# A transformer block in split float32: the activations tile H moves behind the small constants

## The chip, the cores and the metric

The kernel runs on one core of one Trainium2 chip. The metric is the device time of one execution in microseconds (us). A matmul here is one TensorE (PE) instruction: its stationary operand (up to 128 columns) is loaded by a weight load (PEld), and then its moving operand (up to 512 columns) is streamed through.

## The reference

One block of a transformer on x[512, 2048], in float32:

```
h    = rms_norm(x, pre_mix_norm)
proj = h @ w_in                          # queries, keys, values, gates
mix  = [diff_attention(8 heads), nsa_attention(8 heads, 2 groups)]
x    = x + rms_norm(mix @ w_out, post_mix_norm)
h    = rms_norm(x, pre_ffn_norm)
u    = causal_dwconv(h @ w_up)           # 2 x 5632 columns, width 3
gate, up = split(u)
y    = (gelu(gate) * up) @ w_down        # 5632 -> 2048
x    = x + rms_norm(y, post_ffn_norm)
```

## The kernel before

Every large product is made of three matmuls on operands split into a high part and a low part (type float32r): high by high, high by low, low by high. ScalarE (ACT) makes the high part with a copy (line 132), VectorE (DVE) the low part with a subtraction (line 133); all matmuls of this kind are issued by the helper mm (line 73).

The tile H holds the activations of a stage, transposed and split: 128 partitions by [2, 16, 512] float32, so 64 KB in each partition. H[:, 0, c] and H[:, 1, c] are the high and the low part of the 128 rows c of the contraction, 2048 bytes per partition each. It is filled four times: with the normed x (lines 202 and 203), with the attention's output (mix_ahead, lines 132 and 133), with the second norm's output (lines 763 and 764), and at the very end with weights of the last part of the down projection (hold_split, lines 132 and 133).

The other operands lie in two pools. "weights" has raw (3 buffers), hi and lo (2 each) of 4096 bytes per partition: raw receives 512 KB of weights by a DMA of SP's queue, hi and lo are its split. "slots" has 37 slots s of 2048 bytes (queries, keys, values, gated activations and much else) and 4 buffers pt of 6656 bytes (13 times 512).

The stages, and which operand H is in each (in `mm(out, stationary, moving)`):

- moving() with the weights wdv, wvs and wvg: H is stationary, the weight tile moves.
- stationary() with wst (queries and keys) and wu (the up projection): the weight tile is stationary, H moves. Between the wst matmuls a queue of small items (scores, transposes, products with values) is worked off; tick() starts one after every few matmuls, so that runs of wst matmuls are broken up. The items of the up projection use no TensorE.
- out_pass() with wo, two token halves: H is stationary, the weight tile moves.
- first_pairs(): the first 4 of the 88 column tiles of the up projection, in pieces of 256 columns.
- down() with wd: the stationary operand is a slot (gated activations), the moving one a weight tile. H takes no part. There are 10 such stages of 192 matmuls, each after a stretch of the up projection.
- The last group of the down projection runs the same down_mms, but its weights lie in H: a slot is stationary, H moves.

The inner loops, all through mm (line 73):

```python
# stationary(): 48 matmuls into one bank
h = hi[:, c * 128:(c + 1) * 128]
mm(b, h, H[:, 0, cc], cc == 0, False)
mm(b, h, H[:, 1, cc], False, False)
mm(b, lo[:, c * 128:(c + 1) * 128], H[:, 0, cc], False, cc == KC - 1)
...
# down_mms(): the slot moves on by token tile, the weights by 2048 bytes
mm(b, gh[:, ts], hi[:, w], first and c == 0, False)
mm(b, gh[:, ts], lo[:, w], False, False)
mm(b, gl[:, ts], hi[:, w], False, last and c == 1)
...
# last_mms(): the same call, hi and lo are now parts of H
hi = H[:, 0, m:m + 2].rearrange("p a b -> p (a b)")
```

Within a pool tiles are laid out in the order in which they are first asked for, each rounded up to 32 bytes. "consts" comes first, and H is its first tile; 15 small constants follow, and gcol is asked for last. The start addresses in a partition (bytes), as the built program has them:

```
tile                          address    mod 2048
H                               16512         128
ident ... vcl, gcol    82048 to 94496     various
raw, hi, lo           94560 to 119136         352
s (37 slots)         123232 to 196960         352
pt (4)               199008 to 218976         352, 864, 1376, 1888
```

Column slices of 128 float32 move a start by 512 bytes, so operands cut from hi, lo, s and pt start at 352 modulo 512 (except some slices of queries of the compressed branch), those cut from H at 128 modulo 512.

Of the kernel before, what the change touches and what calls it, by code (L numbers as in the profile page):

```python
# [13 lines left out]
F = mybir.dt.float32  # L14
R = mybir.dt.float32r
# [6 lines left out]
KC = D // 128  # L22
# [28 lines left out]
def body(ctx, tc, xT, x, gpre, vecs, lam4, tab, onehot, cmpm, wst, wdv, wvs, wvg, w1, w2, wo, wu, wd,  # L51
         gpost, gffn, gpff, out):
    nc = tc.nc
    cp = ctx.enter_context(tc.tile_pool(name="consts", bufs=1))
# [17 lines left out]
    def mm(o, a, b, start, stop):  # L72
        T.matmul(o, a, b, start=start, stop=stop, skip_group_check=True)  # L73

    H = cp.tile([128, 2, KC, 512], R, name="H")
    ident = cp.tile([128, 128], F, name="ident")
    vec = cp.tile([128, V_N], F, name="vec")
    half = cp.tile([128, 4], F, name="half")
# [9 lines left out]
    kcl = cp.tile([128, NKV, 32], R, name="kcl")  # L88
    vch = cp.tile([32, NKV, 128], R, name="vch")
    vcl = cp.tile([32, NKV, 128], R, name="vcl")  # L90
    rv = dp.tile([16, RW], F, name="rv")
    rows_b = dp.tile([16, 128, RW], F, name="rows_b")
    park = dp.tile([PARK, 128, 512], F, name="park")
# [4 lines left out]
    pace = {"rate": 2.0, "credit": 0.0, "now": 0, "ticks": 0, "hold": 0}  # L98

    def step():  # L100
        """one half step: even ones start an item and run second stages, odd ones run the later stages"""
        now = pace["now"] = pace["now"] + 1
        if now % 2:
            run = [f for f in flying if f[1] >= 2 and now - f[2] >= (LAG if f[1] == 2 else 1)]
        else:
            run = [f for f in flying if f[1] == 1]
            if pending and pace["ticks"] >= pace["hold"]:
                run.insert(0, [pending.popleft(), 0, now])
                flying.append(run[0])
        for f in run:  # L110
            f[0][f[1]]()
            f[1] += 1
            f[2] = now
        flying[:] = [f for f in flying if f[1] < len(f[0])]
# [73 lines left out]
                 start=start if k == 0 else None, after=(lambda: evac(box["b"])) if last else None)  # L188
            c0 += n

    # ---- norm of x, transposed and split
    xraw = {}

    def load_x(c0, n):
# [31 lines left out]
            T.transpose(b[:, t * 128:(t + 1) * 128], rstd[:, t:t + 1].to_broadcast([128, 128]), ident)  # L226
        A.activation(rstd_b, b, AF.Copy)

    # ---- tables
    def tables():  # L230
        tb = st.tile([33, 16], F, name="tb")
        oh = sp.tile([33, RW], F, name="oh", tag="pt", bufs=4)
# [32 lines left out]
            V.tensor_copy(kcl[:, :, 31], z)  # L265
        return [bias, lam]

    # ---- evacuations
    def evac_dmajor(scale, hi, lo):
        def f(b):  # L270
            t = slot()
# [4 lines left out]
    LO, UP = slice(0, 64), slice(64, 128)  # L276

    def evac_twins(h, b):
        """keys of the two maps, each twice on the partitions, and their low parts"""
        t = slot()  # L280
        V.tensor_tensor(t, b, rstd_b, OP.mult)
        k0, k1, kl = hold["k", h] = [slot(R) for _ in range(3)]
        A.activation(k0, t, AF.Copy)
        A.activation(k1[UP], t[UP], AF.Copy)
        V.tensor_tensor(kl, t, k0.bitcast(F), OP.subtract)
        nc.gpsimd.dma_start(k0[UP], k0[LO])
        nc.gpsimd.dma_start(k1[LO], k1[UP])

    def evac_stack(h, b):
        """queries of the two maps, high and low parts stacked on the partitions"""  # L290
        t = slot()
        V.scalar_tensor_tensor(t, b, 0.125, rstd_b, op0=OP.mult, op1=OP.mult)
        q0, q1 = hold["q", h] = [slot(R) for _ in range(2)]
        A.activation(q0[LO], t[LO], AF.Copy)
        A.activation(q1[UP], t[UP], AF.Copy)
        V.tensor_tensor(q0[UP], t[LO], q0[LO].bitcast(F), OP.subtract)
        V.tensor_tensor(q1[LO], t[UP], q1[UP].bitcast(F), OP.subtract)
# [7 lines left out]
                V.scalar_tensor_tensor(lo, banks[t][:, :n], r, hi.bitcast(F), op0=OP.mult, op1=OP.subtract)  # L305
        return f

    # ---- attention
    OFF = [0, 384, 768, 1152]
    bias_tiles = {}  # L310

# [4 lines left out]
        bias_tiles[h] = bt  # L316

    def softmax_items(maps, bt, combine, pts):
        """one softmax over the four query tiles; each map is a list of products of queries and keys"""
        zs, nm, sm = {}, {}, {}  # L320

        def scores(i):
            n = 128 * (i + 1)
            qs = slice(i * 128, (i + 1) * 128)
            zs[i] = []
            m = stat(2)
            s = sm[i] = stat(2)
            bs = [bank() for _ in maps]
            for p in range(len(maps[0])):
                for b, ops in zip(bs, maps):  # L330
                    mm(b[:, :n], ops[p][0][:, qs], ops[p][1][:, :n], p == 0, p == len(ops) - 1)
            for j, b in enumerate(bs):
                z = slot()
                zs[i].append(z)
                V.tensor_tensor_reduce(out=z[:, :n], in0=b[:, :n], in1=bt[:, 384 - 128 * i:384 - 128 * i + n],  # L335
                                       scale=-1.0, scalar=3e38, op0=OP.add, op1=OP.min, accum_out=m[:, j:j + 1])
                A.activation(z[:, :n], z[:, :n], AF.Exp, bias=m[:, j:j + 1], scale=-1.0, accum_out=s[:, j:j + 1])  # L337

        def norm(i):
            n = 128 * (i + 1)  # L340
            s = sm[i][:, :len(maps)]
            V.tensor_scalar(s, s, TINY, None, op0=OP.max)
            V.reciprocal(s, s)
            combine(i, n, zs[i], s)

        def turn(i):
            n = 128 * (i + 1)
            o = slice(OFF[i], OFF[i] + n)
            for z, pt in zip(zs.pop(i), pts):
                b = bank()  # L350
                for j in range(i + 1):
                    T.transpose(b[:, j * 128:(j + 1) * 128], z[:, j * 128:(j + 1) * 128], ident)  # L352
                split(pt[0][:, o], pt[1][:, o], b[:, :n])

        return [[lambda i=i: scores(i), lambda i=i: norm(i), lambda i=i: turn(i)] for i in (3, 2, 1, 0)]
# [2 lines left out]
        return [sp.tile([128, 1664], R, name="pt", tag="pt", bufs=4) for _ in range(2)]  # L358

    def weighted(b, vh, vl, pt, first, last):  # L360
        """b[e, q] += v^T p^T over the key tiles"""
        for j in range(NT):
            o = b[:, j * 128:]
            def view(t):
                return t[:, :1664].rearrange("p (a b) -> p a b", b=128)[:, 4 * j:4 * j + 3 * (NT - 1 - j) + 1:3]
            f = first and j == 0
            mm(o, vh(j), view(pt[0]), f, False)
            mm(o, vh(j), view(pt[1]), False, False)
            mm(o, vl(j), view(pt[0]), False, last and j == NT - 1)
# [118 lines left out]
        cl[-1] += [lambda: av(0), lambda: (av(1), done())]  # L488
        return cl

    # ---- phase 1: projections and attention
    make_identity(nc, ident)
    V.memset(half, -0.5)
    A.activation(stat(1), half[:, :1], AF.Exp)
# [2 lines left out]
    wb = bank()  # L497
    for _ in range(3):
        T.matmul(wb, ident, warm, start=True, stop=True)
    gcol = cp.tile([128, KC], F, name="gcol")  # L500
    nc.sync.dma_start(gcol, gpre)
    nc.gpsimd.dma_start(vec, vecs)
    bgl = tables()
# [184 lines left out]
    units[-1]["start"] = lambda: start_out()  # L688
    units[-1]["each"] = lambda n: mix_ahead(n - 1) if n else None

    # ---- phase 2: output projection in two token halves, residual, second norm
    msum = st.tile([128, NT, 4], F, name="msum")
    x2sum = st.tile([128, NT, 4], F, name="x2sum")
    mg = {}
# [115 lines left out]
        if n % 3 != 1:  # L810
            u["start"] = lambda n=n: (early_split if n % 3 else early_fetch)(n // 3)

    # ---- phase 3: gated feed-forward
    conv = {}
    gact = {}
    y = {}
# [91 lines left out]
        early[HELD[e]] = hs, ls  # L908

    def first_pairs():  # L910
        """the first two pairs, on the tokens that are ready first and then on the rest"""
        banks = {}

        def part(key, cols):
            j, which, k = key
            hs, ls = early[key]
            if (j, which) not in banks:
                banks[j, which] = bank()
            b = banks[j, which][:, cols]
            for c in range(8):  # L920
                cc = k * 8 + c
                o = slice(c % 4 * 128, c % 4 * 128 + 128)
                mm(b, hs[c // 4][:, o], H[:, 0, cc, cols], cc == 0, False)
                mm(b, hs[c // 4][:, o], H[:, 1, cc, cols], False, False)
                mm(b, ls[c // 4][:, o], H[:, 0, cc, cols], False, cc == KC - 1)
                if c % 2:
                    yield

        for e in (6, 7):
            def mms(hi, lo, e=e):  # L930
                early[HELD[e]] = [[v[:, o:o + 512] for o in (0, 512)] for v in (hi, lo)]
                for key in HELD[:6] if e == 6 else []:
                    yield from part(key, slice(0, 256))
                yield from part(HELD[e], slice(0, 256))

            def start():
                pace["rate"] = 1.0

            def after():
                flush()  # L940
                for key in HELD:
                    for _ in part(key, slice(256, 512)):
                        pass
                early.clear()
                pace["rate"] = 2.0
                for j in range(2):
                    for which in range(2):
                        up_evac(j, which)(banks.pop((j, which)))
                rows.clear()
            j, which, k = HELD[e]  # L950
            unit(wu[(j * 2 + which) * 2 + k], 1024, mms, start=start if e == 6 else None, after=after if e == 7 else None)
            units[-1]["late"] = e == 7
# [8 lines left out]
            if G and j == G * GROUP:  # L961
                down(G - 1)

    # ---- the weight stream
    raws, his = {}, {}

    def fetch(i):
# [83 lines left out]
    while deferred:  # L1051
        deferred.pop(0)()

    # ---- last group of the down projection, token tiles outermost; its weights take the place of the activations
    gp = row(gpff)
    hold_fetch(2)
    for m in range(4):
# [76 lines left out]


def _halves(w, k=8):
    """[2048, n * 128] to [n * 2, 128, 8 * 128]: column tiles with the rows of a half on the partitions"""
    n = w.shape[1] // 128
    return w.reshape(2, 8, 128, n, 128).transpose(3, 0, 2, 1, 4).reshape(n * 2, 128, 1024)

# [45 lines left out]
```

## Time and profile before

| what | value |
|---|---|
| time, median of 2 runs | 2373.7 us (2372.87 to 2374.53) |
| profiled execution, first to last instruction | 2371.7 us |
| matmuls | 10956, PE busy 2346.8 us (99%) |
| weight loads | PEld busy 1914.7 us (81%) |
| VectorE, ScalarE, GpSimd busy | 54%, 38%, 4% |
| mean granted TensorE clock | 0.998 of full speed |

The profiled span stands beside the median with 2.0 us between them, which lie outside the first and the last instruction. Matmuls are pipelined: one is on record for some 390 ns, while the next starts long before it ends, so what a matmul costs is read from the distance between starts, not from its duration. Names: `b<-H,hi` is a matmul into a bank b of PSUM whose operands are H and hi, with no order between them; which one moves is told by the code. A name with hi covers the matmuls that read the high part of the weights, one with lo those that read the low part.

### The profile page before, as it was taken

To read this page: it belongs to the slowest core of one execution; us is meant where nothing else is said; L and a number is where in the kernel's file an instruction comes from. 1 tells how busy PE (TensorE), PEld (TensorE's weight loads), DVE (VectorE), ACT (ScalarE), POOL (GpSimd) and SP (SyncE) were. 2 spreads that over 40 slices of the span, in tenths; PEclk is the share of its full clock that TensorE was granted. 3 is DMA by queue.
4 is the path that set the end of the run, shared out by engine and by line. 5 is a ranking of instruction groups with operands and counts; after the bars stand their busy time and mean duration, and the time that the engine had idled before them with its cause. 6 is when DMAs were issued, how large, how long until landed. Compare 5 with 4: busy or idle time off the path is not lost.

```text
span 2371.7 us, 28580 instructions
## 1 busy us (share of the span) xinstructions
PE 2346.8 (99%) x10956; PEld 1914.7 (81%) x10956; DVE 1289.3 (54%) x2454; ACT 892.5 (38%) x1823; POOL 89.9 (4%) x145
## 2 busy tenths in 40 slices
PE   9999999999999999999999999999999999999997
PEld 7877778988887769788888888888888888888886
DVE  5266665657785565544545444544545454544556
ACT  6245553444464453323232332323232232323233
POOL 1001100000010101000000000000000000000002
PEclk9999999999999999999999999999999999999999
DMA  8433333432246562222322222222222222222325
GB/s 302 153 94 100 96 97 116 152 110 63 72 155 227 204 234 87 98 98 89 100 96 97 93 95 93 96 96 92 103 90 98 98 89 98 98 89 98 116 89 186
DMA packets 81689, 276.09 MB, mean 116 GB/s; under 512 B 9914, under 2 KB 9914, under 8 KB 81552
## 3 DMA queue, kind: packets, MB, share of 16 engines
q1 hardware_dynamic: 72000, 243.51, 30.1%
q0 software_dynamic: 9552, 30.76, 4.0%
q8 instruction: 86, 1.41, 0.2%
q14 instruction: 51, 0.42, 0.1%
HBM read 260.29 MB, written 17.08 MB: 117 GB/s over the span
## 4 chain that ended last, share of the span: by engine, by line
PE 91%; DVE 3%; DMA 3%; issue 1%; ACT 1%; SPq 0%; POOL 0%; DVEq 0%; ACTq 0%; POOLq 0%
PE b L73 90%; DMA raw<-wo 1%; PE b L352 1%; DVE lo L133 1%; DMA s<-xpark 1%; ACT hi L132 0%; DMA raw<-wdv 0%; DVE s L1090 0%; DMA raw<-wd 0%; DVE H L133 0%; DVE pt L133 0%; PE b L759 0%; DVE s L827 0%; DVE s L826 0%; PE b L413 0%
## 5 line engine op out<-in xcount | busy, mean ns | idle before, releaser
L73 PE MATMUL b<-H,hi 128*128 128x512 f32 (+1 forms) x3776 | 1187.8, 396 | 0.0
L133 DVE TENSOR_TENSOR lo<-raw,hi 128x512 fp32r<-128x512 f32 (+1 forms) x808 | 534.7, 686 | 776.1 <-ACT hi L132 775.4
L73 PEld LDWEIGHTS b<-H,hi 128*128 128x128 f32 x3776 | 696.1, 188 | 163.6 <-issue 3.5
L132 ACT ACTIVATE hi<-raw 128x512 fp32r<-128x512 f32 (+1 forms) x808 | 472.4, 621 | 930.3 <-PE b L73 772.7
L73 PE MATMUL b<-H,lo 128*128 128x512 f32 (+1 forms) x1888 | 741.9, 393 | 0.1
L73 PEld LDWEIGHTS b<-H,lo 128*128 128x128 f32 x1888 | 353.9, 187 | 86.2 <-DVE lo L133 1.1
L73 PE MATMUL b<-hi,s 128*128 128x512 f32 x1280 | 396.0, 389 | 0.0
L73 PE MATMUL b<-hi,H 128*128 128x512 f32 (+2 forms) x1024 | 299.0, 371 | 5.0 <-ACT hi L132 4.9
L73 PEld LDWEIGHTS b<-hi,s 128*128 128x128 f32 x1280 | 240.3, 188 | 50.2
L73 PE MATMUL b<-lo,s 128*128 128x512 f32 x640 | 249.0, 389 | 0.0
L73 PEld LDWEIGHTS b<-hi,H 128*128 128x128 f32 x1024 | 185.1, 188 | 42.5 <-ACT hi L132 9.8
L73 PE MATMUL b<-lo,H 128*128 128x512 f32 (+2 forms) x512 | 190.4, 372 | 3.7 <-DVE lo L133 3.4
L73 PEld LDWEIGHTS b<-lo,s 128*128 128x128 f32 x640 | 120.2, 188 | 25.1
L870 DVE TENSOR_TENSOR s<-s,b 128x512 f32<-128x512 f32 x160 | 107.4, 685 | 43.7 <-PE b L73 41.7
L73 PEld LDWEIGHTS b<-lo,H 128*128 128x128 f32 x512 | 96.3, 188 | 26.0 <-DVE lo L133 10.4
L337 ACT ACTIVATE s<-s,st 128x512 f32<-128x512 f32 (+3 forms) x128 | 71.0, 556 | 106.9 <-DVE st L335 106.9
L132 ACT ACTIVATE s<-s 128x512 fp32r<-128x512 f32 (+1 forms) x72 | 42.0, 583 | 118.3 <-DVE s L846 63.3
L73 PEld LDWEIGHTS b<-pt,s 128*128 128x128 f32 (+1 forms) x480 | 69.0, 166 | 6.1
L73 PE MATMUL b<-pt,s 128*62 128x256 f32 (+3 forms) x480 | 73.5, 302 | 0.0
L335 DVE CUSTOM_DVE_ANT_0 s<-b,bt 128x512 f32<-128x512 f32 (+3 forms) x128 | 57.6, 487 | 29.4 <-PE b L73 28.9
L133 DVE TENSOR_TENSOR s<-s 128x512 fp32r<-128x512 f32 (+1 forms) x72 | 45.5, 632 | 46.8 <-ACT s L132 46.8
L73 PE MATMUL b<-H,s 128*128 128x256 f32 (+1 forms) x384 | 67.9, 337 | 0.0
(185 smaller groups left out, 1444.0 us busy)
## 6 DMA issues: line engine op xcount, KB each, us to landing
raw<-wu SPq DMA_DIRECT2D x176, 512.0 KB, 3.2
raw<-wd SPq DMA_DIRECT2D x88, 512.0 KB, 3.2
raw<-wst SPq DMA_DIRECT2D x64, 512.0 KB, 3.5
raw<-wo SPq DMA_DIRECT2D x64, 512.0 KB, 3.3
raw<-w SPq DMA_DIRECT2D x16, 512.0 KB, 4.3
raw<-wdv SPq DMA_DIRECT2D x15, 512.0 KB, 6.6
rows_b<-rv POOLq DMA_DIRECT2D x1, 5120.0 KB, 24.2
s<-xT SPq DMA_DIRECT2D x16, 256.0 KB, 6.1
```

What stands on the lines that cost most here:

```text
L73: T.matmul(o, a, b, start=start, stop=stop, skip_group_check=True)
L132: A.activation(hi, src, AF.Copy)
L133: V.tensor_tensor(lo, src, hi.bitcast(F), OP.subtract)
L335: V.tensor_tensor_reduce(out=z[:, :n], in0=b[:, :n], in1=bt[:, 384 - 128 * i:384 - 128 * i + n], scale=-1.0, scalar=3e38, op0=OP.add, op1= ...
L337: A.activation(z[:, :n], z[:, :n], AF.Exp, bias=m[:, j:j + 1], scale=-1.0, accum_out=s[:, j:j + 1])
L352: T.transpose(b[:, j * 128:(j + 1) * 128], z[:, j * 128:(j + 1) * 128], ident)
L870: V.tensor_tensor(y[t, g], y[t, g], b, OP.add)
```

## The change

H is asked for after the other constants instead of before them; gcol, which was asked for last, is now asked for just ahead of H. No instruction is added, removed or moved on any engine. The further hunks of the diff only take out comments and docstrings.

```diff
@@ -72,7 +72,6 @@
-    H = cp.tile([128, 2, KC, 512], R, name="H")
     ident = cp.tile([128, 128], F, name="ident")
     vec = cp.tile([128, V_N], F, name="vec")
...
@@ -88,6 +87,8 @@
     vch = cp.tile([32, NKV, 128], R, name="vch")
     vcl = cp.tile([32, NKV, 128], R, name="vcl")
+    gcol = cp.tile([128, KC], F, name="gcol")
+    H = cp.tile([128, 2, KC, 512], R, name="H")
     rv = dp.tile([16, RW], F, name="rv")
...
@@ -497,7 +498,6 @@
     for _ in range(3):
         T.matmul(wb, ident, warm, start=True, stop=True)
-    gcol = cp.tile([128, KC], F, name="gcol")
     nc.sync.dma_start(gcol, gpre)
```

The addresses after it: H at 29024, which is 352 modulo 2048. The small constants move down by 65536 bytes (32 times 2048), so each keeps its own offset modulo 2048; weights, slots, pt and all later tiles stay where they were.

## Rows read from the trace of the kernel before

**Rows 1.** The page: span, busy time, granted clock in 40 slices

```profile
span 2371.7 us, 28580 instructions
...
PE 2346.8 (99%) x10956; PEld 1914.7 (81%) x10956; DVE 1289.3 (54%) x2454; ACT 892.5 (38%) x1823; POOL 89.9 (4%) x145
...
PEclk9999999999999999999999999999999999999999
```

**Rows 2.** PE groups by form (busy, mean ns of one; idle before)

```profile
L73 PE MATMUL b<-H,hi 128*128 128x512 f32 x3712 | 1176.1, 398 | 0.0
L73 PE MATMUL b<-H,lo 128*128 128x512 f32 x1856 | 733.0, 395 | 0.1
...
L73 PE MATMUL b<-hi,H 128*128 128x512 f32 x768 | 249.8, 399 | 5.0 <-ACT hi L132 4.9
...
L73 PE MATMUL b<-lo,H 128*128 128x512 f32 x384 | 153.7, 400 | 3.4 <-DVE lo L133 3.1
L73 PE MATMUL b<-H,s 128*128 128x512 f32 x192 | 45.0, 395 | 0.0
```

**Rows 3.** Timeline of PE, up to down projection (start us, us, instruction)

```profile
1402.18 0.63 PE L73 MATMUL b<-H,hi 128*128 128x512 f32 x2
...
1404.28 0.63 PE L73 MATMUL b<-H,hi 128*128 128x512 f32 x2
...
1404.98 0.40 PE L73 MATMUL b<-hi,s 128*128 128x512 f32 x1
1405.22 0.39 PE L73 MATMUL b<-lo,s 128*128 128x512 f32 x1
1405.44 0.63 PE L73 MATMUL b<-hi,s 128*128 128x512 f32 x2
...
1406.83 0.62 PE L73 MATMUL b<-hi,s 128*128 128x512 f32 x2
...
1436.07 0.62 PE L73 MATMUL b<-hi,s 128*128 128x512 f32 x2
...
1447.63 0.62 PE L73 MATMUL b<-hi,s 128*128 128x512 f32 x2
```

**Rows 4.** Timeline of PE, last stretch of the up projection, then last group

```profile
2247.49 0.63 PE L73 MATMUL b<-H,hi 128*128 128x512 f32 x2
...
2314.70 1.56 PE L73 MATMUL b<-H,s 128*128 128x512 f32 x6
...
2357.63 2.03 PE L73 MATMUL b<-H,s 128*128 128x512 f32 x8
```

**Rows 5.** Timeline of PE, scores (two slots) between wst matmuls

```profile
518.52 0.71 PE L73 MATMUL b<-H,hi 128*128 128x512 f32 x2
...
521.41 1.55 PE L73 MATMUL b<-s 128*128 128x512 f32 x6
522.79 0.63 PE L73 MATMUL b<-H,hi 128*128 128x512 f32 x2
```

**Rows 6.** Windows (us; busy and count of PE, PEld, DVE, ACT, POOL; PEclk, DMA share, GB/s)

```profile
1050.00:1138.00 88.00, 88.00 (x379) 70.70 (x378) 41.27 (x64) 28.89 (x49) 0.00 (x0) 1.00 0.27 93
1407.00:1448.00 41.00, 41.00 (x182) 33.96 (x182) 21.43 (x33) 8.71 (x15) 0.00 (x0) 1.00 0.29 98
20.00:74.00 54.00, 54.00 (x233) 42.64 (x232) 24.72 (x46) 30.81 (x68) 2.65 (x3) 1.00 0.84 302
730.00:860.00 130.00, 125.33 (x535) 96.97 (x536) 82.41 (x136) 69.72 (x141) 9.21 (x15) 1.00 0.58 200
```

**Rows 7.** Chain that ended last, 40 to 150 us (start us, us, what)

```profile
48.82 96.54 PE b L73 x414
```

**Rows 8.** Chain that ended last, 725 to 890 us, long pieces

```profile
732.05 64.45 PE b L73 x275
...
821.69 8.24 DMA raw<-wo
...
875.28 14.73 PE b L73 x65
```

## The prediction

> **What bounds the kernel now.** I read the page first: PE is busy for 2346.8 of 2371.7 us, its granted clock stays at the upper of the two levels (2.4 GHz) in every slice [rows 1]. Then the groups by form: in front of the great matmul groups PE was idle for a few us in all [rows 2]. So a faster DMA or another order can give little here. What remains is the time that one matmul takes from PE, and that is read from the distance between starts.
>
> The timeline has two values for it, with the same shape, clock and count of weight loads. In the up projection (a weight tile stationary, H moving) three matmuls begin every 0.70 us: from 1402.18 to 1404.28 there are nine in 2.10 us, 233.3 ns each. In the down projection (a slot stationary, a weight tile moving) it is 0.68: from 1436.07 to 1447.63 there are 51 in 11.56 us, 226.7 ns each [rows 3]. Which of them a matmul gets goes with H and with nothing else that I can find:
>
> - The last group of the down projection runs the code of down() with H as the moving operand. From 2314.70 to 2357.63 PE starts 184 matmuls (H,s has 192, and the last row, of 8, starts there): 42.93 us, 233.3 each. The stretch of the up projection ahead of it has 288 in 67.21 us, 233.4 [rows 2, 4].
> - With H stationary it is the same: 96.54 us for 414 matmuls of wdv and wst (233.2), 64.45 for 275 of wo (234.4) [rows 7, 8].
> - Load on the other engines doesn't order it. In the slow stretch VectorE is busy for 41.27 of 88 us and ScalarE for 28.89; in the fast one for 21.43 of 41 and 8.71; DMA share is 0.27 and 0.29 [rows 6].
> - The pattern of accumulation doesn't either: 48 matmuls into one bank (up projection) and 3 into each bank in turn (wo) both take 233, the 6 in turn of the down projection 226.7.
>
> What H has that the others lack is its place. Operands cut from hi, lo and the slots start at 352 modulo 512, those cut from H at 128. In every fast pair both offsets are equal, in every slow pair they differ. The 37 slots lie over 74 KB and hi, lo up to 16 KB below them, and all the pairs between them are fast, so distance alone isn't it.
>
> **The change part by part.** It moves no instruction. The small constants keep their offsets modulo 2048; gcol's place costs nothing, since it is only asked for earlier. What is left is that H starts at 352 modulo 2048, so each matmul with H has the same pair of offsets as one of the down projection. I take that these then cost what those do: 233.3 - 226.7 = 6.67 ns less (0.70 against 0.68 us for three, which the two long counts confirm).
>
> The 512-column matmuls with H are 3712 + 1856 + 768 + 384 + 192 = 6912 [rows 2], worth 46.1 us if all of them gain. By stage:
>
> 1. Up projection and last group, 84 x 48 + 192 = 4224 matmuls, unbroken and without a wait: 4224 x 6.67 = 28.2 us. What could come late next is far: DMA share 0.27, VectorE at 41 of 88 us [rows 6]. The split of the last weights into H follows the same matmuls, so it moves with them.
> 2. wdv, 2 x 16 x 4 x 3 = 384 matmuls: 2.6 us. PE is busy for 54.00 of the 54 us from 20 to 74, but the DMA share is 0.84 [rows 6]; were they the bound once PE is 3% faster, this is 0. I take 2.6.
> 3. wo, 768 matmuls: PE misses 4.7 us of 130 there, and the chain has a wait of 8.24 us for wo itself [rows 6, 8]. Where PE waits for that, a faster matmul only waits longer. I count the two unbroken stretches alone, 275 + 65: 340 x 6.67 = 2.3 us; all would be 5.1.
> 4. wst amid attention, 5568 - 4032 = 1536 matmuls in short runs, as the 12 from 518.52 [rows 5]. Here the gain isn't sure to be whole, because an equal pair needs a run-in: the first eight of a down stage take 1.85 us (1404.98 to 1406.83), 231 each, and only then 226.7 [rows 3]. The nearest row for a short run of equal pairs are the scores, slots on both sides: six in 1.38 us, 230.0 [rows 5]. That is 3.3 ns less than 233.3: 1536 x 3.3 = 5.1 us. Whole it would be 10.2, and at worst 0.
> 5. Matmuls of 128 to 280 columns: the trace shows them with and without H in too many forms to tell a difference; I count 0. The 12 us behind the last matmul stay.
>
> The sum is 28.2 + 2.6 + 2.3 + 5.1 = 38.2 us. From the profiled 2371.7 it leaves 2333.5; with the 2.0 us between this span and the median of 2373.7, 2335.5 us.
>
> The Trainium skill speaks against this: "TensorE: Matmul & The Clock Gate", section "Step-by-step: what each phase is for", says that PE has two independent read ports in SBUF, one for the moving operand and one for the weight load, so that a load takes no bandwidth from the running matmul. By it two operands' offsets couldn't matter to each other, and the sum would be 0. The trace disagrees so far as the two values stand in it for one shape, 233.3 and 226.7; that the offsets make the difference no run has shown yet.
>
> **The rivals.**
>
> - *The cost goes with H's region, not with its offset.* H ends 80 KB into a partition before and 92 KB after; all fast operands lie above 104 KB. Then nothing changes: 2373.7 us. For it: no row shows a pair at two equal offsets that includes the low region. Against it: H spans 64 KB and its pairs take 233 in all of it, and the slots span 74 KB without a step, so the border would have to lie in the one gap between H and hi. The Trainium skill's rule of two ports gives the same time.
> - *Only one role gains.* If the offset matters only where H is stationary, 384 + 340 matmuls gain 6.67: 4.8 us, 2369. If only where H moves, items 1 and 4 are left: 33.3 us, 2340, within the forecast's range.
> - *Equal offsets collide, and down() escapes by its order.* The first matmul of a down stage takes 0.24 us (1404.98 to 1405.22), more than any 233, and the next ones fall below it [rows 3]. down() moves on to another column slice of its stationary operand only after six matmuls; stationary() does it after three, and may stay at that first value. At 240 ns instead of 233.3 all 6912 lose 6.7: 46 us, 2420. It decides if a matmul with H goes above 234 at all. Against it: the second matmul of that same run-in starts 0.22 us after the first, and the scores, which change their operands too, have 230.
>
> **How the numbers follow.** The forecast has 0.80: a clean split of all rows by one property, which the change makes equal. The region has 0.12, one role 0.05, the collision 0.03. Low end: all 6912 at 6.67 (46.1 us) and something from the smaller matmuls, 1 to 2 us: 2326. High end: item 1 alone is 28.2 us, 2345.5; if each of the 84 column tiles had a run-in (eight matmuls of 231 instead of 226.7, 0.035 us), 3 us of it are lost: 2349. I give 2325 to 2350, which holds the forecast and part of the one-role case, 0.80 together. A measurement of this kernel tells about 2% from no change, that is 47.5 us, 2326.2: only the last us of the range are below. Faster by over 2% gets 0.06, within it 0.92, slower by over 2% 0.02 (the collision at 241 or more).
>
> **What would show it.** In the changed profile the up projection has 0.68 us for three matmuls, and 88 us of it some 390 matmuls instead of 379; the last group's 184 take 41.7 us; the run-in at the start of a down stage is gone or stays, which says whether it comes from the change of offsets. The wo stage's waits for DMA grow by what PE gains. It is wrong if matmuls with H stay at 233 (region), if only wdv and wo fall (one role), or if any of them rises above 234 (collision).

## The result and the profile after

The changed kernel takes 2335.97 us (median of 2 runs, 2335.62 to 2336.33) against 2373.7: a ratio of 0.9842, 95% interval 0.9814 to 0.9871. The forecast was 2335.5. The gain is 1.6%: clear of no change by the interval, and within the 2% for which the forecast gave 0.92. The profiled execution spans 2333.5 us, 38.2 less than before.

The page of the changed kernel, with the lines of [rows 1]:

```profile
span 2333.5 us, 28580 instructions
...
PE 2307.7 (99%) x10956; PEld 1917.4 (82%) x10956; DVE 1289.6 (55%) x2454; ACT 892.6 (38%) x1823; POOL 90.1 (4%) x145
...
PEclk9999999999999999999999999999999999999999
```

PE is busy for 99% as before, at the same clock: the gain is not a wait that went. The groups of PE by form, as in [rows 2]:

```profile
L73 PE MATMUL b<-H,hi 128*128 128x512 f32 x3712 | 1155.2, 392 | 0.0
L73 PE MATMUL b<-H,lo 128*128 128x512 f32 x1856 | 724.0, 390 | 0.1
...
L73 PE MATMUL b<-hi,H 128*128 128x512 f32 x768 | 245.8, 394 | 4.8 <-ACT hi L133 4.8
L73 PE MATMUL b<-lo,H 128*128 128x512 f32 x384 | 151.7, 395 | 3.8 <-DVE lo L134 3.2
L73 PE MATMUL b<-H,s 128*128 128x512 f32 x192 | 43.7, 389 | 0.0
```

The same counts, and each form's mean is shorter: from 395 to 389 ns in the last group, the value that the down projection's forms had before and have now. The distance between starts is plain in PE's timeline at the border of the up and the down projection, where [rows 3] had the jump:

```profile
1380.16 0.61 PE L73 MATMUL b<-H,hi 128*128 128x512 f32 x2
...
1384.24 0.61 PE L73 MATMUL b<-H,hi 128*128 128x512 f32 x2
...
1384.92 0.39 PE L73 MATMUL b<-hi,s 128*128 128x512 f32 x1
1385.15 0.39 PE L73 MATMUL b<-lo,s 128*128 128x512 f32 x1
1385.38 0.62 PE L73 MATMUL b<-hi,s 128*128 128x512 f32 x2
...
1387.42 0.62 PE L73 MATMUL b<-hi,s 128*128 128x512 f32 x2
```

From 1380.16 to 1384.24 there are 18 matmuls with H moving in 4.08 us, 226.7 ns each (before: 233.3). The down projection begins at 1384.92 and goes on at once with 0.23, 0.23 us; its run-in of eight matmuls (0.24, 0.22, ... in [rows 3]) is gone. In the chain that ended last, the stretch from 1030 to 1280 us is one piece that holds both projections:

```profile
1029.90 250.24 PE b L73 x1104
```

250.24 us for 1104 matmuls, 226.7 each, whatever their operands. The last group, as in [rows 4]:

```profile
2277.08 1.30 PE L73 MATMUL b<-H,s 128*128 128x512 f32 x5
```

```profile
2317.66 3.11 PE L73 MATMUL b<-H,s 128*128 128x512 f32 x13
```

Of its 192 matmuls the last 13 start from 2317.66 on, so 179 take 40.58 us, 226.7 each (before 233.3). Between attention items, as in [rows 5]:

```profile
511.01 0.71 PE L73 MATMUL b<-H,hi 128*128 128x512 f32 x2
...
511.79 0.62 PE L73 MATMUL b<-H,hi 128*128 128x512 f32 x2
...
512.49 0.62 PE L73 MATMUL b<-H,hi 128*128 128x512 f32 x2
...
513.17 0.61 PE L73 MATMUL b<-H,hi 128*128 128x512 f32 x2
...
513.85 1.52 PE L73 MATMUL b<-s 128*128 128x512 f32 x6
515.21 0.61 PE L73 MATMUL b<-H,hi 128*128 128x512 f32 x2
```

After the small matmuls with kch a wst run needs its run-in: three matmuls take 0.70 us from 511.79 to 512.49, and only then 0.68 (to 513.17) and 0.68 (to 513.85). The scores behind it follow an equal pair and take 1.36 us for six, 226.7 each, where [rows 5] had 1.38. The windows of [rows 6]:

```profile
1050.00:1138.00 88.00, 88.00 (x390) 72.88 (x389) 45.92 (x72) 30.28 (x51) 0.00 (x0) 1.00 0.29 96
1385.00:1426.00 41.00, 41.00 (x183) 33.94 (x182) 21.59 (x34) 10.42 (x18) 0.00 (x0) 1.00 0.28 92
20.00:74.00 54.00, 54.00 (x240) 43.77 (x239) 25.29 (x46) 30.65 (x68) 2.65 (x3) 1.00 0.83 301
730.00:860.00 130.00, 124.76 (x544) 98.23 (x544) 83.25 (x139) 69.35 (x141) 10.86 (x18) 1.00 0.63 212
```

The 88 us from 1050 hold 390 matmuls instead of 379 (their end is now in the down projection, which has the same distance). From 20 to 74 us PE still has no gap. In the window of the wo stage PE misses 5.2 us of 130 instead of 4.7, but the changed kernel runs 8 to 12 us ahead there, so the two windows hold different matmuls; the same matmuls are compared further down. Last, the long pieces of the chain of [rows 7] and [rows 8]:

```profile
47.53 93.99 PE b L73 x414
```

```profile
724.99 60.76 PE b L73 x268
...
810.97 7.03 DMA raw<-wo
```

96.54 us for 414 matmuls became 93.99 (227.0 each), wo's first stretch has 226.7, and the longest wait for wo on the chain is 7.03 instead of 8.24 us.

### The profile page after: what moved, and what is told of

Same layout as the page of the kernel before. It is cut to its first block, busy times and chain, and to the rows that moved or that the text cites. A ratio compares the mean times of both kernels' runs of the same rounds, so it can differ in the third digit from the quotient of the medians.

```text
span 2333.5 us, 28580 instructions
## 1 busy us (share of the span) xinstructions
PE 2307.7 (99%) x10956; PEld 1917.4 (82%) x10956; DVE 1289.6 (55%) x2454; ACT 892.6 (38%) x1823; POOL 90.1 (4%) x145
## 4 chain that ended last, share of the span: by engine, by line
PE 92%; DVE 3%; DMA 3%; issue 1%; ACT 1%; SPq 0%; POOL 0%; DVEq 0%; ACTq 0%; POOLq 0%
PE b L73 90%; DMA raw<-wo 2%; PE b L353 1%; DVE lo L134 1%; DMA s<-xpark 1%; ACT hi L133 0%; DMA raw<-wdv 0%; DVE s L1090 0%; DMA raw<-wd 0%; DVE H L134 0%; DVE pt L134 0%; PE b L759 0%; DVE H L764 0%; DVE s L752 0%; PE b L457 0%
## 5 line engine op out<-in xcount | busy, mean ns | idle before, releaser
L73 PE MATMUL b<-H,hi 128*128 128x512 f32 (+1 forms) x3776 | 1167.2, 391 | 0.0
L73 PE MATMUL b<-H,lo 128*128 128x512 f32 (+1 forms) x1888 | 733.1, 388 | 0.1
L827 DVE SCALAR_TENSOR_TENSOR s<-b,vec,s 128x510 f32<-128x510 f32 x88 | 65.9, 749 | 3.1
```

Source lines behind the costliest of these rows:

```text
L827: V.scalar_tensor_tensor(c[:, 2:], b[:, :510], w[0], c[:, 2:], op0=OP.mult, op1=OP.add)
```

## The experiments

All are edits of the changed kernel that move tiles, with the same instructions in the same order. Each is a single run, unless said otherwise, and stands beside the kernel before on the same chip; seven runs of the kernel before on one chip spread from 2370.97 to 2372.94 us, so a difference of 2 us in one time decides nothing; the distances in the traces decide. For short: the distance is the time from the start of one 512-column matmul to the start of the next. The window from 1050 to 1130 us tells it by its count, which takes in the matmuls that its edges cut (one or two): 80 us hold 343 at 233.3 ns and 353 at 226.7. It lies in the up projection in the kernels with 233.3; in those with 226.7, which run ahead, its end lies in the down projection, which has 226.7 there too. The kernel before, and the changed one:

```profile
1050.00:1130.00 80.00, 80.00 (x344) 1.00 0.27 92
```

```profile
1050.00:1130.00 80.00, 80.00 (x355) 1.00 0.30 99
```

### Is it the start itself, or the region?

```diff
+    pad = cp.tile([128, 72], F, name="pad")
     ident = cp.tile([128, 128], F, name="ident")
```

> The changed kernel with 288 bytes left free ahead of the constants: H, weights, slots and pt all start at 128 modulo 512, where H alone started in the kernel before. Theory 1 (a matmul is fast when its two operands have equal offsets): as the changed kernel, 2336 us, 226.7 ns from matmul to matmul in the up projection and in the down projection. Theory 2 (a start at 128, a multiple of 64 bytes, is slow by itself): all 512-column matmuls take 233.3, also the 1920 of the down projection, 2374 + 1920 x 6.67 ns = 2386 us.

It took 2335.48 us, beside 2370.5 for the kernel before. The window:

```profile
1050.00:1130.00 80.00, 80.00 (x354) 1.00 0.30 99
```

All large tiles at 128 are as fast as all at 352. So a start at 128 is not slow by itself: theory 2 falls. In the next run H is almost where it was before the change, but at an equal offset.

```diff
-    ident = cp.tile([128, 128], F, name="ident")
     vec = cp.tile([128, V_N], F, name="vec")
+    gcol = cp.tile([128, KC], F, name="gcol")
+    H = cp.tile([128, 2, KC, 512], R, name="H")
+    kch = cp.tile([128, NKV, 32], R, name="kch")
     half = cp.tile([128, 4], F, name="half")
+    ident = cp.tile([128, 128], F, name="ident")
...
-    gcol = cp.tile([128, KC], F, name="gcol")
-    H = cp.tile([128, 2, KC, 512], R, name="H")
```

> H lies low again (18272 to 83808, before: 16512 to 82048), but at 352 modulo 512, with only vec and gcol ahead of it. Theory 1 (equal offsets): 2336 us, 226.7 ns in the up projection. Rival (the region in which H lies, or its nearness to the weights, decides): 2374 us, 233.3 ns. H is at 1888 modulo 2048 here, so 2336 us also says that 512 is enough and 2048 isn't needed.

It took 2335.79 us, beside the same 2370.5:

```profile
1050.00:1130.00 80.00, 80.00 (x355) 1.00 0.30 99
```

The region doesn't matter, and equality modulo 512 is enough.

### How equal must the offsets be?

First gcol goes behind H, which then starts at 288 modulo 512; in the second run kch does, and H starts at 96:

```diff
-    gcol = cp.tile([128, KC], F, name="gcol")
     H = cp.tile([128, 2, KC, 512], R, name="H")
+    gcol = cp.tile([128, KC], F, name="gcol")
```

```diff
-    kch = cp.tile([128, NKV, 32], R, name="kch")
...
     H = cp.tile([128, 2, KC, 512], R, name="H")
+    kch = cp.tile([128, NKV, 32], R, name="kch")
```

> gcol (64 bytes) goes behind H, so H starts at 288 modulo 512 and the rest at 352; nothing else changes. Theory 1 with offsets compared modulo 128 or more: 233.3 ns with H, 2374 us. Theory 1 with offsets compared modulo 64 or less: still equal, 2336 us.

> kch (256 bytes) goes behind H, so H starts at 96 modulo 512 and the rest at 352. Theory 1 with offsets compared modulo 512: 233.3 ns with H, 2374 us. Compared modulo 256 or less: still equal, 2336 us. A price that grows with the distance of the offsets would show here against the 64 bytes: more than 233.3.

With 64 bytes it took 2368.61 us, with 256 bytes 2333.19, beside 2370.5. The windows, first of the one, then of the other:

```profile
1050.00:1130.00 80.00, 80.00 (x345) 1.00 0.28 92
```

```profile
1050.00:1130.00 80.00, 80.00 (x354) 1.00 0.27 92
```

Offsets 256 apart count as equal, 64 apart don't. That the run with 256 bytes is 2 us below the changed kernel is no gain of its own: when the two traces are laid over each other, start by start, the 2.4 us between their spans arise at the beginning and in the wo stage, where PE waits for DMA; from there to the last matmul the distance between them stays at 2.42 us. One thing didn't fit: with 64 bytes the matmuls of wdv, where H is stationary, have another distance than those where H moves:

```profile
50.00:90.00 40.00, 40.00 (x176) 1.00 0.64 222
```

Less the one or two that the edges cut, that is some 229 ns for each, the mean of the steps from start to start. So the next runs looked at more distances, and at the sign. For 128 bytes half, rstd, neglam and sub8 go behind H, for 32 half alone:

```diff
-    half = cp.tile([128, 4], F, name="half")
...
     H = cp.tile([128, 2, KC, 512], R, name="H")
+    half = cp.tile([128, 4], F, name="half")
```

> half, rstd, neglam and sub8 (32 bytes each) go behind H, so H starts at 224 modulo 512 and the rest at 352. The offsets differ by 128. If offsets are compared modulo 256 (the run with 256 bytes was as fast as equal offsets): 233.3 ns with H, 2374 us. If modulo 128: 226.7, 2336 us.

> half (32 bytes) goes behind H, so H starts at 320 modulo 512 and the rest at 352. Theory 1 (any difference within the modulus is slow): 233.3 ns with H in both roles, 2374 us. Rival (sign and size of the difference count, as the 229 of the matmuls with H stationary in the run with 64 bytes suggests): other values than 233.3, and not the same for H moving and H stationary.

They took 2370.46 and 2371.58 us, beside 2373.72. The windows of 128 and of 32 bytes:

```profile
1050.00:1130.00 80.00, 80.00 (x345) 1.00 0.28 94
```

```profile
1050.00:1130.00 80.00, 80.00 (x344) 1.00 0.30 99
```

So 128 apart isn't equal and 256 apart is: the offsets act modulo 256. Below 32 bytes H becomes a view into a larger tile, 4 elements in, and 7 in the other run:

```diff
-    H = cp.tile([128, 2, KC, 512], R, name="H")
+    HW = cp.tile([128, 2 * KC * 512 + 8], R, name="H")
+    H = HW[:, 4:4 + 2 * KC * 512].rearrange("p (a c n) -> p a c n", a=2, c=KC)
```

> The tile of H gets 32 bytes more, and H is a view into it that starts 16 bytes in: H at 368 modulo 512, weights, slots and pt at 384. If any difference of the offsets within 256 bytes costs: 233.3 ns with H, 2374 us. If differences under 32 bytes don't count: 226.7, 2336 us.

> As with 16 bytes, but the view starts 28 bytes in: H at 380, the rest at 384, one float32 apart. If any difference costs: 233.3 ns with H, 2374 us. If the price grows with the difference from zero: between 226.7 and the value of the run with 16 bytes. If differences under 16 or 32 bytes don't count: 226.7, 2336 us.

They took 2370.33 and 2357.57 us, beside 2372.11 for the kernel before. The windows, 16 bytes first:

```profile
1050.00:1130.00 80.00, 80.00 (x345) 1.00 0.28 94
```

```profile
1050.00:1130.00 80.00, 80.00 (x348) 1.00 0.29 93
```

With H moving even one float32 costs, though less (230.8). The mean distances of all these kernels, worked out from the starts of the 512-column matmuls in the traces (steps over 260 ns left out; the up projection behind 930 us, wdv up to 115 us):

| H lies below the rest by (modulo 256) | up projection, H moving | wdv, H stationary | time |
|---|---|---|---|
| 0 (changed kernel) | 226.7 | 226.9 | 2335.97 |
| 0 (256 bytes) | 226.7 | 226.9 | 2333.19 |
| 4 | 230.8 | 231.1 | 2357.57 |
| 16 | 233.5 | 227.4 | 2370.33 |
| 32 | 233.3 | 233.3 | 2371.58 |
| 64 | 233.3 | 229.0 | 2368.61 |
| 128 | 233.3 | 232.4 | 2370.46 |
| 224 (kernel before) | 233.3 | 233.3 | 2373.7 |

The times come from several chips, on which the kernel before took 2370.5 to 2373.7 us.

Only equality gives 226.7 in both roles. But unequal pairs can have it too, and some of the means hide that. With 4 bytes, wdv's 231.1 is a mixture: the 124 matmuls from 14.53 to 42.41 us have 226.7, the 221 from 47.48 to 98.81 have 233.3. With 16 bytes it is 228.3 for the former and 226.8, as good as equal, for the latter. Two windows in this second part of wdv, with 4 and then with 16 bytes:

```profile
52.00:92.00 40.00, 40.00 (x173) 1.00 0.61 208
```

```profile
50.00:90.00 40.00, 40.00 (x178) 1.00 0.65 223
```

And with 16 bytes a stretch of the up projection, from 957.19 to 1001.68 us, has 236.7, while all later ones have 233.3. So equality is enough for 226.7, but it is not the only way to it, and the size of the difference alone doesn't set the price.

### Is it H at all?

A pad of 64 bytes becomes the first tile of the slots' pool, and kch, half, rstd, neglam, sub8 and gcol go behind H:

```diff
+    pad = sp.tile([128, 16], F, name="pad")
     ident = cp.tile([128, 128], F, name="ident")
...
     H = cp.tile([128, 2, KC, 512], R, name="H")
+    kch = cp.tile([128, NKV, 32], R, name="kch")
...
```

> 64 bytes are left free ahead of the slots, and H goes with the slots: H, s and pt at 416 modulo 512, raw, hi and lo at 352. Now the down projection has unequal operands (s stationary at 416, weights moving at 352) and its last group equal ones (s and H). Theory 1: the down projection rises from 226.7 to 233.3, its last group stays at 226.7, though H moves there; the up projection rises to 233.3 too, or to about 229 if the sign counts (weights 64 bytes below H, as for H stationary in the run with 64 bytes); 2366 to 2386 us. Rival (H is what is slow, wherever it lies apart from 352): the down projection stays at 226.7 and the last group is at 233.3.

It took 2373.56 us, as much as the kernel before (2373.72). The windows: an up stage, the down stage after it, the next up stage, the last group:

```profile
1050.00:1130.00 80.00, 80.00 (x344) 1.00 0.28 96
1140.00:1175.00 35.00, 35.00 (x151) 1.00 0.28 91
1185.00:1265.00 80.00, 80.00 (x351) 1.00 0.27 93
2320.00:2355.00 35.00, 35.00 (x156) 1.00 0.48 159
```

The down projection, in which H has no part, has become slow: 151 matmuls in 35 us, where the last group has 156 in the same 35 us. The mean distances are 233.3 and 226.7, the reverse of the kernel before. So H was never what was slow; its pairs were unequal. The timeline at the border from up to down, 1135.37, shows that the down stage keeps the 0.70 us for three:

```profile
1134.67 0.63 PE L73 MATMUL b<-H,hi 128*128 128x512 f32 x2
...
1135.37 0.39 PE L73 MATMUL b<-hi,s 128*128 128x512 f32 x1
...
1135.84 0.63 PE L73 MATMUL b<-hi,s 128*128 128x512 f32 x2
...
1136.54 0.63 PE L73 MATMUL b<-hi,s 128*128 128x512 f32 x2
```

### Where does the run-in come from?

```diff
-    ident = cp.tile([128, 128], F, name="ident")
     vec = cp.tile([128, V_N], F, name="vec")
+    gcol = cp.tile([128, KC], F, name="gcol")
+    ident = cp.tile([128, 128], F, name="ident")
...
-    gcol = cp.tile([128, KC], F, name="gcol")
     H = cp.tile([128, 2, KC, 512], R, name="H")
```

> vec and gcol go ahead of ident, so that ident starts at 352 modulo 512 as slots, weights and H do; H stays as in the changed kernel. Theory A (a run-in follows a change of the pair's offsets, here from transposes with ident at 128): wst matmuls between attention items fall from a mean of 229.3 to 227 ns, about 1475 x 2.5 ns = 4 us, 2332 us. Theory B (a run-in follows whatever breaks the stream of 512-column matmuls): 229.3 stays, 2336 us.

It took 2337.65 us beside 2373.72, and its wst matmuls amid attention have the mean distance of the changed kernel: 229.2 against 229.1 over the 1420 steps up to 260 ns (229.3 in both if steps up to 280 are taken in). A window in the attention of the differential heads, first of this kernel, then of the changed one:

```profile
160.00:360.00 200.00, 200.00 (x973) 1.00 0.34 97
```

```profile
160.00:360.00 200.00, 200.00 (x974) 1.00 0.33 97
```

973 against 974, where theory A, with 659 wst matmuls in the window, would have added some 8: it falls for the transposes. The other small operands (kch among them) kept their offsets, so this run alone doesn't settle it for those.

The trace of the changed kernel goes further. Behind scores of 512 columns, both operands in slots, 10 of 13 runs of wst matmuls have no run-in: 226 or 227 ns from the second step on, as in the run that starts at 515.21 (above). Behind scores of 384, 256 or 128 columns, both operands in slots too, all 38 runs have one: from 384 columns the steps go, for instance, 231, 231, 236, 228, 232, 231 and only then 227. So where all pairs are equal, the run-in follows narrower matmuls, which is theory B. The run-in of the down stage in [rows 3] was another case: it followed 512-column matmuls of an unequal pair, and went when that pair became equal. Why the stream needs these matmuls to settle no run shows.

### The size, once more

The changed kernel without any edit, in more runs.

> The changed kernel itself against the kernel before, on one chip, to narrow the interval of the ratio: theory (6912 matmuls, of which all but those in short runs and at waits gain 6.67 ns, 38 us of 2373): 0.984. No rival; it is here for the size.

2334.98 us (median of 4 runs) against 2372.11 (7 runs): ratio 0.9841, interval 0.9825 to 0.9858.

## Why the prediction was right

The step on which all rested, that equal offsets of the two operands give a matmul the 226.7 ns of the down projection, holds: H alone was moved, and the 512-column matmuls with H went from 233.3 to 226.7 wherever nothing breaks the stream; the pad of 288 bytes, the low H and the shifted slots show that neither the start itself nor the region nor H decides. The prediction took the offsets modulo 512; the runs with 128 and 256 bytes say modulo 256. One of its rows proves less than it says: of the 414 matmuls that it counts for H stationary only 221 are wdv; 180 are wst, where H moves. Wdv alone had 233.3 too, as the table above shows.

The terms, against the two traces laid over each other: the n-th matmul is the same in both, so for each form the steps from start to start can be subtracted and summed.

| term | predicted | measured |
|---|---|---|
| up projection, 4032 | 26.9 | 26.2 |
| last group, 192 | 1.3 | 1.3 |
| wdv, 384 | 2.6 | 2.0 |
| wo, 768 | 2.3 | 4.1 |
| wst amid attention, 1536 | 5.1 | 5.6 |
| narrower matmuls with H, 768 | 0 | -1.5 |
| all other matmuls | 0 | 1.3 |
| from the last matmul's start to the end | 0 | -0.7 |
| sum (predicted with its rounding) | 38.2 | 38.2 |

So the exact hit has luck in it, for errors of 2 us cancel.

- The up projection and the last group gave nearly what they should; of the 0.7 us that the up projection lacks, 0.4 lie in breaks of its first stretch (steps over 260 ns). Wdv lacks 0.6, of which 0.4 lie in such breaks at its beginning.
- wo is the term that was mis-sized, and its reason failed. The forecast counted the two stretches that no wait breaks (2.3 us) and gave the rest to the waits for DMA: a faster matmul would only wait longer. But the waits didn't grow. Over the same matmuls, the steps above 260 ns hold 14.8 us more than 233.3 each before, and 14.7 more than 226.7 each after. 4.1 of the possible 5.1 us arrived, and the missing 1.0 lies in the 711 other steps: 228.1 on the mean, since the runs behind a break begin with a run-in.
- wst: the nearest row, the scores, said 3.3 ns for each; it was 3.6. The reason for taking less than 6.67 was right (a run-in), its cause wasn't known, and the transposes' offsets aren't it. That the row fitted so well is partly chance: those scores had 230.0 behind an unequal pair of 512 columns, and have 226.7 in the changed kernel, while the run-in of wst comes behind narrower matmuls.
- Narrower matmuls were counted at 0 and cost 1.5 us; see below.

The rivals: the region falls with the low H; one role alone falls, since wdv (226.9) and the up projection (226.7) both came down; the collision falls, no long stretch with H is above 227. The Trainium skill's rule in "TensorE: Matmul & The Clock Gate", section "Step-by-step: what each phase is for", that the two read ports of PE are independent and a weight load takes no read bandwidth from the running matmul, was read by the prediction as no change. The measurement decides against that reading in this kernel: with the same instructions, 226.7 or 233.3 ns go with where the two operands start. Whether the read ports, the memory or something else in the chip does that no run shows.

## What to carry to other kernels

Where PE is busy all the time, compare the distance between starts of equal matmuls from stage to stage: if one shape has two values, look at where the operands start. For 512-column float32 matmuls with a weight load each, let both operands of TensorE start at the same offset modulo 256 bytes: no other choice tried here gave 226.7 in every stage. It costs an order of allocation or a pad, and was worth 6.67 ns in 233.3 here. A small tile among the constants shifts everything behind it, as gcol with its 64 bytes did here. For narrower matmuls see the end of the next section.

## What was not expected

**An unequal pair has several steady values, and a stage keeps the one it falls into.** In the run with shifted slots the ten up stages behind the first alternate: from 1045.8 us 233.3, from 1180.2 228.9, from 1312.9 233.3, and so on to the end, with the same code and offsets in each (344 and 351 matmuls in 80 us, in the windows above). Equal pairs had 226.7 in every up and down stage of these runs, breaks left out and once through a run-in. The runs with 4 and 16 bytes show the same: one part of wdv at one value and the next, behind a few small matmuls, at another. The sign of the difference counts as well: where the moving operand lay 64 bytes above the stationary one, the values were 228.9 or 233.3 (wdv with 64 bytes, the up projection with shifted slots); where it lay 64 below, they were 233.3 alone. A run-in may be the same thing, some eight matmuls until the stream has found its value; that is a reading of the steps, not shown.

**Narrower matmuls like it the other way.** In first_pairs 96 matmuls of 256 columns (a slot stationary, H moving) took from 920.70 to 931.90 us before, 116.7 ns each:

```profile
920.70 11.36 PE L73 MATMUL b<-H,s 128*128 128x256 f32 x96
931.90 0.40 PE L73 MATMUL b<-H,hi 128*128 128x256 f32 x2
```

and from 909.22 to 920.74 after, 120.0 each:

```profile
909.22 11.68 PE L73 MATMUL b<-H,s 128*128 128x256 f32 x96
920.74 0.40 PE L73 MATMUL b<-H,hi 128*128 128x256 f32 x2
```

The same 96 have 120.0 in every run with equal pairs, and also with H 128 bytes below the slots. With H 64 bytes below they took 113.3:

```profile
915.70 11.04 PE L73 MATMUL b<-H,s 128*128 128x256 f32 x96
926.58 0.39 PE L73 MATMUL b<-H,hi 128*128 128x256 f32 x2
```

There are 768 matmuls of 256 and 280 columns with H, so it is 1.5 us here; in a kernel of 256-column matmuls equal offsets might cost rather than gain, which wasn't tried.
